# Image contrast on one core: one tile for six buffers, a first tile in two pieces, two double loads

## The chip, the cores and the metric

The kernel runs on one core of a Trainium2 chip. The metric is the device time of one execution in microseconds (us), as the median of several runs. TensorE (PE) multiplies matrices, VectorE (DVE) and ScalarE (ACT) work on rows of data, GpSimd (POOL) sets constants here, and SyncE (SP) only issues transfers. Transfers between the chip's memory and the on-chip buffers are carried by 16 DMA engines, which all issuing engines share. On-chip data lie in 128 partitions.

## The reference

The input is a batch of 16 images with 3 planes of 512 x 512 float32 values. Each of the 48 planes is pulled away from its own mean by a factor and clipped:

```python
def reference(x, factor):                      # x: (16, 3, 512, 512), factor 1.5
    mean = np.mean(x, axis=(2, 3), keepdims=True)
    return np.clip(mean + factor * (x - mean), 0, 1).astype(np.float32)
```

Every value is read once and written once: 50.33 MB in and 50.33 MB out. The mean of a plane must be known before its first value can be written.

## The kernel before

**Tiling.** The input is seen as a flat row of numbers, cut into rows of 8192 (`ROW`, 32 KB). One plane fills 32 such rows. A tile is 128 rows, one per partition, so it holds 4 whole planes and 4 MiB (4.194 MB). There are 12 tiles, numbered from 0. Six buffers of 32 KB per partition hold them (`BUFS`, pool `xpool`; a buffer is taken in `load`, line 64).

**Load** (lines 63 to 66). SP issues one transfer per tile. The first six are issued ahead of all work (lines 100 and 101); the load of tile t + 6 is issued after the work on tile t is written down (lines 104 and 105), and waits until the store of tile t has landed, since it takes its buffer.

**Compute** (lines 68 to 94). The sum of each row is shared by two engines: DVE reduces columns 0 to 4351 (line 71), ACT copies columns 4352 to 8191 into a scratch tile and accumulates their sum on the way (line 75). Two small matmuls with a block matrix that holds (1 - factor) / (512 * 512) add the 32 rows of each plane and hand the result to all of them (lines 79 and 80); the second matmul waits for the DVE sum. DVE copies this bias out (line 82). Then the tile is rewritten in place in column pieces: ACT computes relu(factor * x + bias) (line 88), DVE takes the minimum with 1 (line 89). Tile 0 has three pieces of 2048, 3072 and 3072 columns (`FIRST`), every other tile two of 5120 and 3072 (`CHUNKS`).

**Store** (lines 96 and 97). ACT issues the stores. Tile 0 is stored in three transfers: its first 2048 columns, written down after the second piece, then 3072 and 3072 columns. Every other tile is stored by one transfer after its last piece. ACT's queue is in order, so a store that waits also holds back the ACT work on the next tile.

**What sets the order.** The kernel is written in Tile, a layer that derives the waits between engines and transfers from the tiles that they touch; `manual_schedule` keeps the order in which the instructions are written down on each engine. SP's queue holds only the loads, ACT's queue the activations and the stores. Both queues of transfers run on the same 16 DMA engines. A transfer of a tile is cut by rows: one packet per row and partition, 32 KB for whole rows, 8 or 12 KB for the pieces of tile 0's stores.

Of the kernel before, what the change touches and what calls it, by code (L numbers as in the profile page):

```python
# [1 line left out]

# [4 lines left out]


P = 128  # L10
ROW = 8192
BUFS = 6
CHUNKS = (5120, 3072)
FIRST = (2048, 3072, 3072)
SUM = 4352


@with_exitstack
def kernel(
    ctx: ExitStack,  # L20
    tc: tile.TileContext,
    x: bass.AP,
    factor: float,
    out: bass.AP,
):


    nc = tc.nc
    f32 = mybir.dt.float32
    Alu = mybir.AluOpType  # L30
    Act = mybir.ActivationFunctionType

    B, C, H, W = x.shape
    n_img, n_pix = B * C, H * W
    ppi = n_pix // ROW
    per_tile = P // ppi
    n_tiles = n_img // per_tile
    assert ppi * ROW == n_pix and per_tile * n_tiles == n_img

    factor = float(factor)  # L40
    wconst = (1.0 - factor) / float(n_pix)

    x_f = x.rearrange("b c h w -> (b c h w)")
    out_f = out.rearrange("b c h w -> (b c h w)")

    def dram(ap, t, c0=0, c1=ROW):
        return bass.AP(tensor=ap.tensor, offset=t * P * ROW + c0, ap=[[ROW, P], [1, c1 - c0]])

    consts = ctx.enter_context(tc.tile_pool(name="consts", bufs=1))
    xpool = ctx.enter_context(tc.tile_pool(name="xpool", bufs=BUFS))  # L50
    jpool = ctx.enter_context(tc.tile_pool(name="jpool", bufs=1))
    rpool = ctx.enter_context(tc.tile_pool(name="rpool", bufs=2))
    bpool = ctx.enter_context(tc.tile_pool(name="bpool", bufs=2))
    psum = ctx.enter_context(tc.tile_pool(name="psum", bufs=2, space=bass.MemoryType.PSUM))

    blockw = consts.tile([P, P], f32, name="blockw")
    nc.gpsimd.memset(blockw, 0.0)  # L57
    for a in range(0, P, ppi):
        nc.gpsimd.memset(blockw[a : a + ppi, a : a + ppi], wconst)  # L59

    tiles = {}

    def load(t):
        xt = xpool.tile([P, ROW], f32, name="xt")
        nc.sync.dma_start(out=xt, in_=dram(x_f, t))  # L65
        tiles[t] = xt

    def compute(t):
        xt = tiles[t]
        sums = rpool.tile([P, 2], f32, name="sums")  # L70
        nc.vector.tensor_reduce(  # L71
            out=sums[:, 0:1], in_=xt[:, 0:SUM], axis=mybir.AxisListType.X, op=Alu.add
        )
        junk = jpool.tile([P, ROW - SUM], f32, name="junk")
        nc.scalar.activation(  # L75
            out=junk, in_=xt[:, SUM:ROW], func=Act.Copy, accum_out=sums[:, 1:2]
        )
        pbias = psum.tile([P, 1], f32, name="pbias")
        nc.tensor.matmul(pbias, blockw, sums[:, 1:2], start=True, stop=False)  # L79
        nc.tensor.matmul(pbias, blockw, sums[:, 0:1], start=False, stop=True)  # L80
        bias = bpool.tile([P, 1], f32, name="bias")
        nc.vector.tensor_copy(out=bias, in_=pbias)  # L82

        chunks, pieces = (FIRST, True) if t == 0 else (CHUNKS, False)
        c, done = 0, 0
        for n in chunks:
            part = xt[:, c : c + n]
            nc.scalar.activation(out=part, in_=part, func=Act.Relu, bias=bias, scale=factor)  # L88
            nc.vector.tensor_scalar(out=part, in0=part, scalar1=1.0, scalar2=None, op0=Alu.min)  # L89
            if pieces and c > 0:  # L90
                store(t, done, c)
                done = c
            c += n
        store(t, done, ROW)

    def store(t, c0, c1):
        nc.scalar.dma_start(out=dram(out_f, t, c0, c1), in_=tiles[t][:, c0:c1])  # L97

    with tc.manual_schedule():
        for t in range(min(BUFS, n_tiles)):  # L100
            load(t)
        for t in range(n_tiles):
            compute(t)
            if t + BUFS < n_tiles:
                load(t + BUFS)


# [1 line left out]
_INS = ['x', 'factor']  # L109
_OUTS = [((16, 3, 512, 512), 'float32')]  # L110

_NUMBERS = {'factor': 1.5}


# [26 lines left out]
```

## Time and profile before

| | |
|---|---|
| median of 6 runs | 240.02 us (239.57 to 240.24) |
| profiled execution | 239.52 us, of which the profile's span is 237.3 us |
| traffic | 100.67 MB, mean 424 GB/s over the span |
| ACT busy | 131.2 us (55%) |
| DVE busy | 111.9 us (47%) |
| PE busy | 14.0 us (6%) |
| load queue (q1) | 1728 packets, 12 transfers of 4096 KB |
| store queue (q10) | 2016 packets, 11 transfers of 4096 KB, 2 of 1536 KB, 1 of 1024 KB |

The span runs from the first to the last instruction of the profiled execution. Times inside it are counted from its start. Some 2.2 us of the execution lie around the span. Busy shares of engines are means over the whole span; a share of the DMA engines counts all 16. A transfer's issue and its landing are far apart, because transfers queue: a load lands a median of 33.9 us after its issue, a store of a whole tile 50.4 us after it. The packets include 16 small ones per transfer that report its completion, which is why 12 loads of 128 rows make 1728 packets.

### The profile page before, as it was taken

The page shows a single profiled execution, that of the slowest core. Times are in us where ns is not written, and L with a number is a line of the kernel's source. Part 1 is how long each engine was busy: PE and PEld are TensorE (multiplying, and loading weights), DVE is VectorE, ACT ScalarE, POOL GpSimd, SP SyncE. Part 2 cuts the span into 40 slices and gives each one's busy share as a digit, 9 for nine tenths or more (in the row PEclk, how much of TensorE's full clock was granted, in tenths as well). Part 3 has the DMA queues.
Part 4 walks back from the last instruction along what each step waited for, and adds up shares of the span by engine and source line. Part 5 has one row for each costly group of instructions (what it writes and reads, how often), then busy time and mean ns, then how long its engine had stood idle before and what let it go on. Part 6 is the DMA issues. An engine that isn't in the chain of part 4 may idle for free.

```text
span 237.3 us, 310 instructions
## 1 busy us (share of the span) xinstructions
PE 14.0 (6%) x48; PEld 12.0 (5%) x48; DVE 111.9 (47%) x49; ACT 131.2 (55%) x50; POOL 0.9 (0%) x9
## 2 busy tenths in 40 slices
PE   0000010100101001010010010001001001000000
PEld 0000010100101001010010010001001001000000
DVE  0072855919468293782764282562734627330000
ACT  2058678586785967769379059256536806900000
POOL 1000000000000000000000000000000000000000
DMA  7999998989999999999999999999999999999996
GB/s 265 442 442 442 420 447 379 472 387 447 453 442 425 420 392 442 442 442 442 442 442 442 436 405 409 431 442 442 442 442 436 442 442 403 425 414 442 442 442 265
DMA packets 3745, 100.67 MB, mean 424 GB/s; under 512 B 416, under 2 KB 416, under 8 KB 416
## 3 DMA queue, kind: packets, MB, share of 16 engines
q1 hardware_dynamic: 1728, 50.33, 49.6%
q10 hardware_dynamic: 2016, 50.33, 49.2%
q14 instruction: 1, 0.01, 0.0%
HBM read 50.33 MB, written 50.33 MB: 424 GB/s over the span
## 4 chain that ended last, share of the span: by engine, by line
DMA 39%; another core or an unknown queue 24%; DVE 12%; ACT 10%; issue 2%; PE 1%; SPq 0%; ACTq 0%
DMA xt<-in_x_dram 19%; DMA out_dram<-xt 19%; ACT xt L88 9%; DVE xt L89 6%; DVE sums L71 5%; ACT junk L75 1%; PE pbias L80 1%; SPq L65 0%; PE pbias L79 0%; DVE bias L82 0%; ACTq L97 0%; ACTq L88 0%; ACTq L75 0%
## 5 line engine op out<-in xcount | busy, mean ns | idle before, releaser
L88 ACT ACTIVATE xt<-xt,bias 128x3072 f32<-128x3072 f32 (+2 forms) x25 | 87.9, 3566 | 21.0 <-DVE bias L82 13.6
L89 DVE TENSOR_SCALAR xt<-xt 128x3072 f32<-128x3072 f32 (+2 forms) x25 | 54.3, 2208 | 56.1 <-ACT xt L88 56.1
L71 DVE TENSOR_REDUCE sums<-xt 128x1 f32<-128x4352 f32 x12 | 56.2, 4682 | 33.8 <-DMA xt<-in_x_dram 33.8
L75 ACT ACTIVATE junk<-xt 128x3840 f32<-128x3840 f32 x12 | 40.9, 3404 | 55.3 <-DMA xt<-in_x_dram 41.8
L79 PE MATMUL pbias<-sums,blockw 128*128 128x1 f32 x24 | 7.0, 361 | 183.7 <-ACT junk L75 183.7
L79 PEld LDWEIGHTS pbias<-sums,blockw 128*128 128x128 f32 x24 | 6.0, 310 | 184.7 <-ACT junk L75 167.9
L80 PE MATMUL pbias<-sums,blockw 128*128 128x1 f32 x24 | 7.0, 362 | 2.9 <-DVE sums L71 2.5
L80 PEld LDWEIGHTS pbias<-sums,blockw 128*128 128x128 f32 x24 | 6.0, 311 | 3.9 <-DVE sums L71 3.4
L82 DVE COPY bias<-pbias 128x1 f32<-128x1 f32 x12 | 1.9, 158 | 8.1 <-PE pbias L80 8.1
L75 ACT ACTIVATION_READ_ACCUMULATOR junk<-xt 128x1 f32 x12 | 2.3, 188 | 0.0
L75 ACT ACT_TABLE_LOAD x1 | 1.3, 1283 | 0.7 <-PEq L122 0.7
L59 POOL MEMSET blockw<- 32x32 f32 x4 | 0.5, 118 | 0.2
L57 POOL MEMSET blockw<- 128x128 f32 x1 | 0.2, 204 | 0.3 <-POOLq L122 0.3
L122 POOL MEMSET const-bfloat16-1.0<- 128x1 bf16 x1 | 0.1, 111 | 0.0
L122 POOL MEMSET const-uint8-127<- 128x1 uint8 x1 | 0.1, 111 | 0.0
L122 POOL MEMSET const-float32-1.0<- 128x1 f32 x1 | 0.1, 108 | 0.0
L122 POOL MEMSET const-float32-0.0<- 128x1 f32 x1 | 0.1, 103 | 0.2 <-issue 0.2
## 6 DMA issues: line engine op xcount, KB each, us to landing
xt<-in_x_dram SPq DMA_DIRECT2D x12, 4096.0 KB, 33.9
out_dram<-xt ACTq DMA_DIRECT2D x11, 4096.0 KB, 50.4
out_dram<-xt ACTq DMA_DIRECT2D x2, 1536.0 KB, 30.8
out_dram<-xt ACTq DMA_DIRECT2D x1, 1024.0 KB, 15.4
```

The costliest lines, as they stand in the source:

```text
L57: nc.gpsimd.memset(blockw, 0.0)
L59: nc.gpsimd.memset(blockw[a : a + ppi, a : a + ppi], wconst)
L71: nc.vector.tensor_reduce(out=sums[:, 0:1], in_=xt[:, 0:SUM], axis=mybir.AxisListType.X, op=Alu.add)
L75: nc.scalar.activation(out=junk, in_=xt[:, SUM:ROW], func=Act.Copy, accum_out=sums[:, 1:2])
L79: nc.tensor.matmul(pbias, blockw, sums[:, 1:2], start=True, stop=False)
L80: nc.tensor.matmul(pbias, blockw, sums[:, 0:1], start=False, stop=True)
L82: nc.vector.tensor_copy(out=bias, in_=pbias)
L88: nc.scalar.activation(out=part, in_=part, func=Act.Relu, bias=bias, scale=factor)
L89: nc.vector.tensor_scalar(out=part, in0=part, scalar1=1.0, scalar2=None, op0=Alu.min)
L122: nc = _bacc.Bacc("TRN2", target_bir_lowering=False, num_devices=1)
```

## The change

The six buffers become one tile `ring` of 128 x 6 x 8192 values, and tile t uses its part t modulo 6. `load` takes a range of columns and a number of tiles. Tile 0 is loaded by two transfers, columns 0 to 2047 (8 KB per row) and 2048 to 8191 (24 KB per row). Tile 1 is loaded by one transfer as before. Tiles 2 and 3 come with one transfer of 8 MiB, tiles 4 and 5 with another; tiles 6 to 11 with one each as before. Tile 0 is stored by two transfers with the same cut as its load; the first of them stands where it stood, and the second, of 24 KB per row, comes after the last piece. The arithmetic, the pieces in which it is done and all other stores are as before. There are 11 loads and 13 stores in place of 12 and 14.

```diff
-FIRST = (2048, 3072, 3072)
+SHORT = 2048
+FIRST = (SHORT, 3072, 3072)
...
-    xpool = ctx.enter_context(tc.tile_pool(name="xpool", bufs=BUFS))
+    xpool = ctx.enter_context(tc.tile_pool(name="xpool", bufs=1))
...
-    tiles = {}
-    def load(t):
-        xt = xpool.tile([P, ROW], f32, name="xt")
-        nc.sync.dma_start(out=xt, in_=dram(x_f, t))
-        tiles[t] = xt
+    ring = xpool.tile([P, BUFS, ROW], f32, name="ring")
+    def load(t, c0=0, c1=ROW, n=1):
+        b = t % BUFS
+        src = bass.AP(
+            tensor=x_f.tensor,
+            offset=t * P * ROW + c0,
+            ap=[[ROW, P], [P * ROW, n], [1, c1 - c0]],
+        )
+        nc.sync.dma_start(out=ring[:, b : b + n, c0:c1], in_=src)
     def compute(t):
-        xt = tiles[t]
+        xt = ring[:, t % BUFS, :]
...
-        chunks, pieces = (FIRST, True) if t == 0 else (CHUNKS, False)
-        c, done = 0, 0
-        for n in chunks:
+        c = 0
+        for n in FIRST if t == 0 else CHUNKS:
             part = xt[:, c : c + n]
             nc.scalar.activation(out=part, in_=part, func=Act.Relu, bias=bias, scale=factor)
             nc.vector.tensor_scalar(out=part, in0=part, scalar1=1.0, scalar2=None, op0=Alu.min)
-            if pieces and c > 0:
-                store(t, done, c)
-                done = c
+            if t == 0 and c == FIRST[0]:
+                store(t, 0, c)
             c += n
-        store(t, done, ROW)
+        store(t, FIRST[0] if t == 0 else 0, ROW)
     def store(t, c0, c1):
-        nc.scalar.dma_start(out=dram(out_f, t, c0, c1), in_=tiles[t][:, c0:c1])
+        nc.scalar.dma_start(out=dram(out_f, t, c0, c1), in_=ring[:, t % BUFS, c0:c1])
     with tc.manual_schedule():
-        for t in range(min(BUFS, n_tiles)):
-            load(t)
+        load(0, c1=SHORT)
+        load(0, c0=SHORT)
+        load(1)
+        load(2, n=2)
+        load(4, n=2)
         for t in range(n_tiles):
             compute(t)
             if t + BUFS < n_tiles:
                 load(t + BUFS)
```

## The prediction

> **What bounds the kernel now.** I read the page's rates first, because this kernel does little arithmetic for 100.67 MB of traffic.
>
> ```profile
> span 237.3 us, 310 instructions
> ...
> DMA  7999998989999999999999999999999999999996
> GB/s 265 442 442 442 420 447 379 472 387 447 453 442 425 420 392 442 442 442 442 442 442 442 436 405 409 431 442 442 442 442 436 442 442 403 425 414 442 442 442 265
> ...
> q1 hardware_dynamic: 1728, 50.33, 49.6%
> q10 hardware_dynamic: 2016, 50.33, 49.2%
> ```
>
> The reader is to see that the 16 DMA engines are busy in every slice but the first and the last: 49.6% of loads and 49.2% of stores make 98.8% of the span. ACT is at 55% and DVE at 47%. The slices scatter, since a packet is counted where it starts, so I asked for the rate in long stretches. Columns: the stretch, the busy time of PE, PEld, DVE, ACT and POOL, the clock, the DMA share, GB/s.
>
> ```profile
> 25.00:65.00 40.00, 3.52 (x12) 3.00 (x12) 25.24 (x12) 28.54 (x12) 0.00 (x0) 1.00 1.01 429
> 100.00:195.00 95.00, 5.86 (x20) 5.00 (x20) 47.77 (x21) 54.05 (x20) 0.00 (x0) 1.00 1.00 433
> ```
>
> 433 GB/s is the working rate, with one load and one store beside each other. 100.67 MB at 433 is 232.5 us. The remaining 4.8 us of the span are: about 1.4 lost in the first 2.5 us (197 GB/s there, 0.59 MB short), 1.0 at the end (the last store, issued at 210.06, lands 26.3 later at 236.3; the span ends at 237.3), 0.4 in the stretch 25 to 65 (4 GB/s times 40 us is 0.16 MB), and small pieces of a few tenths. So a change of order can win at most this little; it loses wherever both DMA queues run empty.
>
> Next, how the two queues share, by single stores' time from issue to landing (one line from each of three answers for the store's line, with the landing under it).
>
> ```profile
> L97 ACTq DMA_DIRECT2D out_dram<-xt x1: 374/374/374, 22.0 to 22.0; - x1
> DMA to landing us min/median/max: 15.4/15.4/15.4
> L97 ACTq DMA_DIRECT2D out_dram<-xt x1: 339/339/339, 25.2 to 25.2; - x1
> DMA to landing us min/median/max: 25.6/25.6/25.6
> L97 ACTq DMA_DIRECT2D out_dram<-xt x1: 338/338/338, 28.0 to 28.0; - x1
> DMA to landing us min/median/max: 36.1/36.1/36.1
> ```
>
> The three pieces of tile 0 land at 37.4, 50.8 and 64.1. So 1.573 MB (12 KB of each row) took 13.4 and 13.3 us: 117 to 118 GB/s. Store 1, with whole rows of 32 KB, was issued at 42.6 and landed 40.9 later, at 83.5: 4.194 MB in 19.4 us, 216 GB/s. Both are what alternation of one row's piece per queue gives: 433 x 12/(12+32) = 118, 433 x 32/64 = 216. I use this rule; for 8 KB it gives 87, and 1.049 MB in 12.1 us, so that store 0's first piece moved from 25.3 to 37.4.
>
> Last, the pace of a tile and what holds a store back.
>
> ```profile
> 42.50 4.68 DVE L71 TENSOR_REDUCE sums<-xt 128x1 f32<-128x4352 f32 x1
> 57.25 0.34 ACTq L97 DMA_DIRECT2D out_dram<-xt  x1
> 127.70 4.51 DVE L89 TENSOR_SCALAR xt<-xt 128x5120 f32<-128x5120 f32 x2 [4.69 <-ACT xt L88]
> 136.85 4.68 DVE L71 TENSOR_REDUCE sums<-xt 128x1 f32<-128x4352 f32 x1 [4.65 <-DMA xt<-in_x_dram]
> 136.90 0.34 ACTq L97 DMA_DIRECT2D out_dram<-xt  x1
> 210.06 0.34 ACTq L97 DMA_DIRECT2D out_dram<-xt  x1
> ```
>
> A tile takes 14.75 us from its first reduction to the issue of its store (42.50 to 57.25), less than the 19.4 in which the DMA moves one tile in and one out. The store of tile 7 was ready at 132.2 and went out at 136.9, when load 8 landed: a store can wait for a load with which it shares no data. Store 11 goes out at 210.06; store 10 lands at 226.7. The last store is thus queued 16.6 us before its turn. That reserve is what the change must not use up.
>
> **The change part by part.** Named l0 to l11 for loads and s0 to s11 for stores by tile (from 0).
>
> *First load in two pieces.* SP issues one more transfer (0.37 to 0.53 us each among the first loads, in the shadow of 4 us of data that the first megabyte brings at 433 GB/s less the start). The first reduction reads columns 0 to 4351 and the activation 4352 to 8191, so both need the second piece: tile 0 starts at 13.1 as now. Later loads queue behind; none is late by more than the issue, and SP is ahead of the DMA. Cost 0; with the cover gone, 0.5 us. I see no gain either: nobody starts on the first piece.
>
> *Store of tile 0 in two pieces, not three.* One ACT issue of 0.34 us goes. The 24 KB piece is issued at 28.0, not its first half at 25.2. At both times s0's first piece still moves (to 37.4), so nothing runs empty. Packets: 128 rows more are cut on the load side, 128 fewer on the store side: 0. Completion packets: two transfers fewer, 32 of 416 small ones: 0. What moves is the sharing: from 37.4 the store gets 433 x 24/56 = 186 GB/s and the loads 247. s0 is out at 37.4 + 3.146/0.186 = 54.3, not 64.1.
>
> *Loads l2+l3 and l4+l5 as one transfer each.* Two SP issues fewer (0.42 to 0.53 us, hidden). Tile 2 now lands with tile 3. Loads by then: 22.8 to 25.3 alone, 1.08 MB; to 37.4 at 346 GB/s, 4.19 MB; the last 3.12 of 8.39 MB at 247 take 12.6 us: l2+l3 land at 50.0. Tile 2 starts at 50.0, not 42.5: 7.5 us late. Who waits: ACT and DVE, then s2, issued at 64.8. The store queue meanwhile has s1 (issued 42.6, moving 54.3 to 73.7), so the 7.5 us cost nothing; without that cover they still cost nothing in DMA time while loads are queued. l4+l5: 1.07 MB until 54.3, 7.32 MB at 216.5: 88.1. Tile 3 is done at 79.5, tile 4 starts 8.6 us later, s4 goes out at 102.9, s5 at 117.6.
>
> *Rest, 19.4 us a tile on each queue.* l6 waits for s0 (54.3) and moves 88.1 to 107.5; l7 to l11 land at 126.9, 146.3, 165.7, 185.1, 204.5. Their slots are free long before: s1 to s5 are out at 73.7, 93.1, 112.5, 131.9 and 151.3, so SP always has a load queued. Stores: s6 170.7, s7 190.1; s8 has 3.1 MB out at 204.5 and then the whole rate: 207.0, s9 216.7, s10 226.4. Tile 11 starts at 204.5 and s11 goes out at 219.3, 7.1 us before its turn, and lands at 236.1. Now it is 236.3. The reserve falls from 16.6 to 7.1 us and the end stays.
>
> *One tile for the buffers.* No instruction changes shape. A gain or a loss could only come from added waits: see the rivals. Its nearest row is the pieces of one buffer now: s0's first piece went out at 21.96, 0.03 us after the last operation on its columns (20.70 + 1.23), while other columns of the same tile were still being written. Columns are told apart inside a tile, so I take 0.
>
> *What no row shows.* How a two-tile load fares per byte: between the 429 of the cut rows and the 433 of whole ones, so 0.4 us either way over 40 us; I take 0, since its rows stay 32 KB. (Should both rows of a partition move as one piece of 64 KB, loads would get two thirds of the rate while the pair lasts, lead the stores by more, and leave a larger reserve; the sum stays.) The start: the same issue and the same first read; between nothing and -0.5 or +0.5 us (one issue); I take 0.
>
> Sum: 0 on a span of 237.3. The profiled execution took 239.52, 2.2 around the span and 0.50 under the median; the other runs scatter from 239.57 to 240.24. I predict the median, **240.0**.
>
> *A rule against the change.* The long stretches hold 433 GB/s with rows 32 KB apart within one load. The Trainium skill, "DMA: Bandwidth & Descriptors", section "Latency and other measured facts", reports that copies whose per-partition rows lie 4 MiB apart fell to 103 GB/s. The double load steps 4 MiB, though only between a partition's two rows. At 103 GB/s its two transfers would take 163 us where 433 gives 39: an estimate from that page of up to 124 us more; no run here shows it yet.
>
> *A rule for a gain.* Through ten tile boundaries between 100 and 195 us the rate stays 433: queued transfers pay nothing for beginning. The same page, section "Anatomy of one DMA", fits a fixed 2 us to each (on another issue path). Two transfers fewer would make 4 us of gain by it, and 0 by the row, which I follow.
>
> **The rivals.**
>
> *A late last store (slower).* Transfers wait for others: s7 above, and one load waited 19.6 us for another load. With 24 transfers in place of 26 the pairs shift. If s9 had to wait for l11, ACT would stand until 204.5: tile 10 ends at 219.2, 2.5 us after s9 is out, and s11 goes out at 233.9, lands 9.7 us later at 243.6: +7.3, about 247.3. It decides once tile 10 starts after 226.4 - 29.5 = 196.9. Against it: s6 and s7 each wait for the very next load now, which ACT needs anyway. Chance 0.10.
>
> *The buffers are no longer told apart (slower).* Were every touch of the one tile ordered, a tile would cost load 9.7 + 14.75 + store 9.7 = 34 us; twelve make 410. The row of s0 speaks against it. 0.03.
>
> *The double loads run slow (slower).* Until 88.1 the two move beside the stores. If all traffic from 22.8 on then ran at 379 GB/s, the lowest slice in the middle, its 28.3 MB would take 74.6 us for 65.3: +9.3, 249.3. The decisive point is a loss of 0.48 us, 0.7% of that stretch. Against it: the low slices stand beside slices of 447 and 472, so they are the scatter of the count. 0.04.
>
> *A real gain.* Without the 0.4 us of the stretch 25 to 65 and an issue's 0.5 at the start: 239.1. For it: that stretch is where the cut rows are. Against: they stay cut. 0.09.
>
> **How the numbers follow.** No change has 0.74, in its own range 239.4 to 240.7 (0.4 us of rate, and the scatter of the runs). 0.2% is 0.48 us, about what a measurement here tells from no change; of the 0.74 I give 0.04 to faster and 0.05 to slower. Faster: 0.09 + 0.04 = 0.13. Slower: 0.10 + 0.03 + 0.04 + 0.05 = 0.22. Same: 0.65. The range 239.1 to 241.1 leaves out nearly all of the three slower rivals (0.17) and a little of the gain.
>
> **What would show it.** After: 433 GB/s from 65 to 195; first reduction at 13.1; the 24 KB store landing near 54; tile 2 starting near 50 and tile 4 near 88; the last load landing near 204 and s11 issued near 219, still before s10 lands. The prediction is wrong if a slice in the middle drops for more than one packet's scatter, if s11 is issued after s10 has landed, or if the first packets come sooner.

## The result

The changed kernel takes 239.27 us (median of 32 runs, 239.0 to 239.92), the kernel before 239.70 (median of 67 runs in the same comparison, 239.52 to 240.73). The ratio is 0.9982, with a 95% interval of 0.9977 to 0.9988: 0.43 us less between the medians. That is inside the 0.2% that the forecast called no change, at 240.0 us in a range of 239.1 to 241.1, yet it is resolved from zero, so there is a small gain to explain.

The profile of the changed kernel, first the page's rates and queues:

```profile
span 238.0 us, 307 instructions
...
DMA  7999999999999999999999999999999999999994
GB/s 308 396 441 441 418 441 410 405 441 441 441 441 435 441 435 441 413 418 413 441 441 441 435 441 441 441 431 435 424 413 413 441 441 441 441 441 435 441 435 193
...
q1 hardware_dynamic: 1840, 50.33, 49.5%
q10 hardware_dynamic: 1872, 50.33, 49.0%
```

The DMA engines are again busy from the second slice to the last but one. The packets have moved as counted: 112 more on the load queue (128 more rows, one transfer fewer), 144 fewer on the store queue (128 rows and one transfer). The profiled execution took 239.90 us, which is one of the longest of its 32, so its span must not be set against the 237.3 of before.

In the two long stretches (columns as before: busy times, clock, DMA share, GB/s):

```profile
25.00:65.00 40.00, 2.35 (x8) 2.01 (x8) 21.27 (x10) 22.94 (x10) 0.00 (x0) 1.00 1.02 432
100.00:195.00 95.00, 7.03 (x24) 6.01 (x24) 53.04 (x24) 62.93 (x24) 0.00 (x0) 1.00 1.00 432
```

The rate is 432 GB/s in both, where it was 429 and 433. The double loads, which move from 22.4 to 86.2 us and so fill the whole first stretch, go as fast as single ones.

The new order, in the timeline of the changed kernel: the first reductions of tiles 0, 2, 4 and 11, and the last store's issue.

```profile
12.78 4.69 DVE L78 TENSOR_REDUCE sums<-ring 128x1 f32<-128x4352 f32 x1 [12.78 <-DMA ring<-in_x_dram]
...
49.38 4.68 DVE L78 TENSOR_REDUCE sums<-ring 128x1 f32<-128x4352 f32 x1 [7.12 <-DMA ring<-in_x_dram]
...
86.22 4.69 DVE L78 TENSOR_REDUCE sums<-ring 128x1 f32<-128x4352 f32 x1 [7.49 <-DMA ring<-in_x_dram]
...
203.37 4.68 DVE L78 TENSOR_REDUCE sums<-ring 128x1 f32<-128x4352 f32 x1 [4.65 <-DMA ring<-in_x_dram]
...
218.10 0.34 ACTq L101 DMA_DIRECT2D out_dram<-ring  x1
```

DVE stands still for 7 us ahead of tiles 2 and 4, waiting for the second tile of a pair that it doesn't need yet, and the last store goes out 8 us later than before. None of this is in the time. Store landings, from single answers for the store's line:

```profile
L101 ACTq DMA_DIRECT2D out_dram<-ring x1: 337/337/337, 27.7 to 27.7; - x1
DMA to landing us min/median/max: 28.0/28.0/28.0
L101 ACTq DMA_DIRECT2D out_dram<-ring x1: 338/338/338, 198.7 to 198.7; - x1
DMA to landing us min/median/max: 28.8/28.8/28.8
L101 ACTq DMA_DIRECT2D out_dram<-ring x1: 338/338/338, 218.1 to 218.1; - x1
DMA to landing us min/median/max: 19.1/19.1/19.1
```

The 24 KB store of tile 0 lands at 55.7, store 10 at 227.5, store 11 at 237.2. Store 11 is queued 9.4 us before its turn.

### The profile page after: what moved, and what is told of

The parts are those of the page before. It is cut to its first block, busy times and chain, and to the rows that moved or that the text cites. A ratio compares the mean times of both kernels' runs of the same rounds, so it can differ in the third digit from the quotient of the medians.

```text
span 238.0 us, 307 instructions
## 1 busy us (share of the span) xinstructions
PE 14.1 (6%) x48; PEld 12.0 (5%) x48; DVE 112.0 (47%) x49; ACT 131.2 (55%) x50; POOL 0.9 (0%) x9
## 4 chain that ended last, share of the span: by engine, by line
DMA 57%; DVE 19%; ACT 10%; another core or an unknown queue 3%; issue 1%; PE 1%; SPq 1%; ACTq 0%
DMA ring<-in_x_dram 40%; DMA out_dram<-ring 16%; ACT ring L93 10%; DVE ring L94 9%; DVE sums L78 9%; PE pbias L87 1%; SPq L73 1%; DVE bias L89 0%; ACTq L93 0%
## 5 line engine op out<-in xcount | busy, mean ns | idle before, releaser
L93 ACT ACTIVATE ring<-ring,bias 128x3072 f32<-128x3072 f32 (+2 forms) x25 | 87.9, 3566 | 22.1 <-DVE bias L89 13.1
L94 DVE TENSOR_SCALAR ring<-ring 128x3072 f32<-128x3072 f32 (+2 forms) x25 | 54.3, 2208 | 56.1 <-ACT ring L93 56.1
L78 DVE TENSOR_REDUCE sums<-ring 128x1 f32<-128x4352 f32 x12 | 56.2, 4683 | 41.8 <-DMA ring<-in_x_dram 41.8
L82 ACT ACTIVATE junk<-ring 128x3840 f32<-128x3840 f32 x12 | 40.9, 3405 | 62.3 <-DMA ring<-in_x_dram 49.0
L82 ACT ACTIVATION_READ_ACCUMULATOR junk<-ring 128x1 f32 x12 | 2.3, 188 | 0.0
## 6 DMA issues: line engine op xcount, KB each, us to landing
out_dram<-ring ACTq DMA_DIRECT2D x1, 1024.0 KB, 16.6
```

The costliest lines, as they stand in the source:

```text
L78: nc.vector.tensor_reduce(out=sums[:, 0:1], in_=xt[:, 0:SUM], axis=mybir.AxisListType.X, op=Alu.add)
L82: nc.scalar.activation(out=junk, in_=xt[:, SUM:ROW], func=Act.Copy, accum_out=sums[:, 1:2])
```

## The experiments

Two questions: what makes the 0.43 us, and is it really the reserve of the last store that decides? For the first, START says that short first rows let data flow earlier (the first reduction stands at 12.78 us, 0.33 earlier). MERGE says that fewer transfers are cheaper. STORE says that tile 0's store in larger pieces is. Ratios are to the kernel before, with 95% intervals. The ratios are given as recorded; they are not the quotients of the medians to the last digit.

### The parts one at a time

*First load cut* (`split_load`, on the kernel before):

```diff
-        nc.sync.dma_start(out=xt, in_=dram(x_f, t))
+        cut = (0, 2048, ROW) if t == 0 else (0, ROW)
+        for c0, c1 in zip(cut, cut[1:]):
+            nc.sync.dma_start(out=xt[:, c0:c1], in_=dram(x_f, t, c0, c1))
```

> The kernel before with one edit: tile 0 is loaded in two pieces of 8 and 24 KB per row. Theory START (the gain is that the first rows are short, so that data flow earlier): the first reduction starts near 12.75 us in place of 13.1, and the time falls by about 0.35 to 0.45 us against the kernel before, ratio 0.998 to 0.9987. Theory MERGE (the gain comes from fewer transfers) and theory STORE (from tile 0's 24 KB store): the time stays, ratio 1.000.

Measured: 239.59 us, 0.9990 (0.9980 to 1.0001); first reduction at 12.97.

*First load whole* (`whole_load`, on the changed kernel):

```diff
-        load(0, c1=SHORT)
-        load(0, c0=SHORT)
+        load(0)
```

> The changed kernel with tile 0 loaded whole again; everything else of the change stays. START: the gain is gone, ratio to the kernel before 1.000 (within 0.0007), first reduction at 13.1 us. MERGE or STORE: the gain stays, 0.998.

Measured: 239.64 us, 0.9999 (0.9990 to 1.0008); first reduction at 12.95, not at 13.1.

*Store of tile 0 in two pieces* (`two_stores`, on the kernel before):

```diff
-            if pieces and c > 0:
+            if pieces and done == 0 and c > 0:
```

> The kernel before with one edit: tile 0 is stored in two pieces of 8 and 24 KB per row, not in three. START and MERGE: ratio 1.000, the last store is issued some microseconds later than 210.06 because stores get a larger share after 37 us. STORE: 0.998.

Measured: 239.68 us, 0.9998 (0.9989 to 1.0007); last store issued at 219.85.

*One tile and double loads alone* (`double_only`, on the kernel before, with the changed kernel's `ring` and `load`, and the three stores of tile 0 kept):

```diff
-        for t in range(min(BUFS, n_tiles)):
-            load(t)
+        load(0)
+        load(1)
+        load(2, n=2)
+        load(4, n=2)
```

> The kernel before with one tile for the buffers and the double loads of tiles 2-3 and 4-5; tile 0 loaded whole and stored in three pieces. START and STORE: ratio 1.000. MERGE: 0.998. If the double step of 4 MiB cost rate, above 1.002.

Measured: 239.62 us, 0.9999 (0.9990 to 1.0008); last store issued at 207.79.

What follows: taking away the cut of the first load takes away the gain, and neither MERGE nor STORE makes one alone. The reserve, too, has an owner. The last store's issue in `two_stores` and in `double_only`:

```profile
219.85 0.34 ACTq L97 DMA_DIRECT2D out_dram<-xt  x1
207.79 0.34 ACTq L102 DMA_DIRECT2D out_dram<-ring  x1
```

In the kernel before it stood at 210.06, 16.6 us before store 10 landed. With the 24 KB store alone store 10 lands at 227.3 and 7.5 us are left; with the double loads alone it lands at 226.8 and 19.0 us are left. It is the larger row of the store, which by the sharing rule takes a larger share of the engines early on, that eats the reserve; the double loads even add to it.

### Pairs, a repeat, and a thinner first piece

`split_two` is `split_load` with the edit of `two_stores`. `split_double` is `double_only` with the first load in two pieces. `after_again` is the changed kernel. `thin_first` is the changed kernel with this edit:

```diff
-        load(0, c1=SHORT)
-        load(0, c0=SHORT)
+        load(0, c1=512)
+        load(0, c0=512)
```

> The changed kernel once more, beside the pairs. The single parts gave 0.9990 (first load in two pieces), 0.9998 (store in two pieces), 0.9999 (double loads) and 0.9999 (both without the first load's cut); their product is 0.9987. If the parts only ADD, this comes out at 0.9985 to 0.999. If the 0.9982 of before holds, two parts work together (PAIR).

> The kernel before with the first load and tile 0's store both in two pieces of 8 and 24 KB per row; six buffers, single loads. ADD: 0.9985 to 0.9992. PAIR with the store: 0.998 to 0.9984. No gain from the start at all: 1.000.

> The kernel before with one tile for the buffers, the first load in two pieces and the double loads; tile 0 stored in three pieces. ADD: 0.9985 to 0.9992. PAIR with the double loads: 0.998 to 0.9984. No gain from the start at all: 1.000.

> The changed kernel, with a first load piece of 2 KB per row instead of 8 (the second is 30 KB); the stores stay. START (short first rows let data flow earlier): as good as the changed kernel or up to 0.15 us better, first reduction at 12.6 to 12.8 us. If the start plays no part: equal to the kernel with tile 0 loaded whole, 0.9999 against the kernel before.

| kernel | first load cut | median us | ratio (interval) | median span of its runs, us | profiled run less its span, us |
|---|---|---|---|---|---|
| before | no | 239.70 | 1 | 237.5 | 2.19 |
| two_stores | no | 239.68 | 0.9998 (0.9989 to 1.0007) | 237.5 | 2.22 |
| double_only | no | 239.62 | 0.9999 (0.9990 to 1.0008) | 237.4 | 2.21 |
| whole_load | no | 239.64 | 0.9999 (0.9990 to 1.0008) | 237.4 | 2.19 |
| split_load | yes | 239.59 | 0.9990 (0.9980 to 1.0001) | 237.8 | 1.89 |
| split_two | yes | 239.43 | 0.9988 (0.9977 to 0.9999) | 237.6 | 1.82 |
| split_double | yes | 239.43 | 0.9988 (0.9979 to 0.9997) | 237.6 | 1.86 |
| thin_first | yes | 239.54 | 0.9993 (0.9985 to 1.0002) | 237.7 | 1.83 |
| after_again | yes | 239.33 | 0.9993 (0.9984 to 1.0001) | 237.5 | 1.85 |
| after | yes | 239.27 | 0.9982 (0.9977 to 0.9988) | 237.4 | 1.86 |

The kernel before has 239.70 in the result's comparison and 239.66 and 239.65 in the two of the other rows; its span here is the median in each of those two, and all spans of that column are recorded to 0.1 us. Every kernel of this table with the cut lies at 0.9982 to 0.9993, every one without at 0.9998 or above. Three of the six intervals still touch 1, and the same program gave 0.9982 and 0.9993, so the size is known only to about 0.1 to 0.4 us. No pair shows more than the cut alone (0.9988 twice), so none is needed, though the intervals do not exclude PAIR by themselves. START falls. The first reductions with the cut stand between 12.78 and 13.00, and `whole_load`, without the cut and without the gain, has 12.95. The first packets start at 1.74 to 1.76 us in every kernel of the table. The thinner piece brings nothing more.

The last column says where to look instead. It is the part of an execution that lies outside the profile's span, before its first instruction or after its last. It is 2.19 to 2.22 us without the cut and 1.82 to 1.89 with it, in the profiled run of every kernel of this case (in all 32 runs of the changed kernel, 1.78 to 1.90). Take it off the medians, and the spans that remain are 237.51 for the kernel before, 237.41 for the changed one and 237.48 for its repeat: the work itself did not become shorter by anything that these runs resolve. In `split_load` and `thin_first` it even became longer: their spans have a mean of 237.78 and 237.70 us, against 237.54 and 237.52 in the runs of the kernel before beside them. What the cut takes off outside the span is there in part given back inside; why, these runs do not show. In the trace, a last 8 KB fetch on the instruction queue begins 1.67 to 1.70 us after the span without the cut and 1.18 to 1.22 after it with the cut, which points to the part behind the last instruction. The fetch moves by some 0.5 us and the time by 0.3 to 0.4, so it is a sign and not the whole account.

Besides the load's own issue and packets, the cut changes one instruction. The first reduction needs both pieces, and its second wait becomes an instruction of its own on DVE's sequencer. The reduction's line in the changed kernel, by line (operations with their count, durations in ns, first and last start):

```profile
L78 DVE TENSOR_REDUCE sums<-ring x12: 4677/4685/4687, 12.8 to 203.4; 128x1 f32<-128x4352 f32 x12
L78 DVEq EVENT_SEMAPHORE  x1: 21/21/21, 12.7 to 12.7; - x1
```

and in `whole_load`, where the second line is missing:

```profile
L78 DVE TENSOR_REDUCE sums<-ring x12: 4677/4683/4687, 12.9 to 202.6; 128x1 f32<-128x4352 f32 x12
its engine sat idle before it (us, times) until:
```

DVE has 62 recorded instructions in every kernel with the cut and 61 in every one without, while the counts of ACT and SP differ within both groups. That the extra instruction moves the end of the program, by where its code falls, fits this, but was not tried, and it is not told apart from the extra load. One dummy wait on DVE in the kernel before would tell.

### How much lateness the end allows

The summing activation of the last tile alone was repeated two or four times, with results that nobody uses, in the changed kernel and in the kernel before (`late_after_2`, `late_after_4`, `late_before_4`):

```diff
+        for _ in range(4 if t == n_tiles - 1 else 0):
+            nc.scalar.activation(out=junk, in_=xt[:, SUM:ROW], func=Act.Copy)
         pbias = psum.tile([P, 1], f32, name="pbias")
```

> The changed kernel with two more passes of the summing activation on the last tile alone, whose results nobody uses: 2 x 3.4 us on ACT before tile 11 is rewritten, so its store goes out near 218.1 + 6.8 = 224.9 us, still before store 10 lands (227.6). RESERVE (an engine's delay costs nothing until the last store is issued after the one before it has landed): time as the changed kernel, 239.3 to 239.7. If compute counted, +6.8: 246.

> The same with four passes: 13.6 us, the last store goes out near 231.7, 4.1 us after store 10 has landed. RESERVE: +4.1 us, and up to 2 us more for the start of a transfer on an empty queue: 243.5 to 245.7. If compute counted in full, +13.6: 253. If it counted nothing, 239.5.

> The kernel before with the same four passes on the last tile: its last store goes out near 210.1 + 13.6 = 223.7, before store 10 lands (226.7). RESERVE: no change, 239.6 to 240.0. If the reserve is not what matters, as late as in the changed kernel: 243.5 to 245.7.

Measured: `late_after_2` 239.33 us, 0.9985 (0.9976 to 0.9995), as the changed kernel. `late_after_4` 243.05 us, 1.0136 (1.0121 to 1.0150). `late_before_4` 239.89 us, 1.0005 (0.9995 to 1.0016). The same 13.7 us of extra ACT work cost 3.7 us in the changed kernel (243.05 against 239.33 in `late_after_2`) and nothing that is resolved in the kernel before. The last store's issue in `late_before_4`:

```profile
221.84 0.34 ACTq L99 DMA_DIRECT2D out_dram<-xt  x1
```

That is still 5.6 us before store 10 lands (227.4). In `late_after_2` it is issued at 222.50, 4.6 us before store 10 lands (227.1). In the timeline and the landings of `late_after_4`:

```profile
206.24 13.71 ACT L86 ACTIVATE junk<-ring 128x3840 f32<-128x3840 f32 x4
...
229.11 0.34 ACTq L103 DMA_DIRECT2D out_dram<-ring  x1
```

```profile
L103 ACTq DMA_DIRECT2D out_dram<-ring x1: 338/338/338, 198.0 to 198.0; - x1
DMA to landing us min/median/max: 28.7/28.7/28.7
L103 ACTq DMA_DIRECT2D out_dram<-ring x1: 338/338/338, 229.1 to 229.1; - x1
DMA to landing us min/median/max: 11.1/11.1/11.1
```

Store 10 lands at 226.7, and store 11 is issued 2.4 us after that. It then takes 11.1 us, where a queued whole tile takes 9.7 (227.5 to 237.2 in the changed kernel): 1.4 us for starting on an idle queue. 2.4 + 1.4 = 3.8, measured 3.7. The issue came 2.6 us earlier than expected: for 2.0 us the extra passes run while ACT would have waited for the bias, and 0.7 us is that tile 11 started at 202.66 here and at 203.37 in the profile of the changed kernel. RESERVE holds in these three kernels: lateness is free up to the landing of the store before, and paid in full from there.

### A version meant to be better

`split_one_store` is `split_load` with tile 0's store in one transfer:

```diff
-        chunks, pieces = (FIRST, True) if t == 0 else (CHUNKS, False)
+        chunks, pieces = (FIRST, False) if t == 0 else (CHUNKS, False)
```

> The kernel before with the first load in two pieces and tile 0's store whole (one transfer, issued near 28 us). No store row is cut. START alone: 0.9988 to 0.9993 like the other kernels with a cut first load. If the small losses of rate between 25 and 65 us come from the cut store rows, they go as well, up to 0.45 us more: 0.997 to 0.9985. If an early store matters to the end: above 1.000.

Measured: 240.08 us, 1.0013 (1.0004 to 1.0022), so it is slower than the kernel before, although its time outside the span is the short one (1.83): the spans of its runs have a median of 238.25 us, against 237.5 in the kernel before and 237.8 in `split_load`. No improvement came; of the three cases, the one above 1.000 did. The reserve is not the reason, since the last store goes out at 223.71, 3.7 us before store 10 lands (227.4). The rate in two stretches of `split_one_store`:

```profile
28.00:36.00 8.00, 1.17 (x4) 1.00 (x4) 4.60 (x2) 6.12 (x3) 0.00 (x0) 1.00 0.97 356
24.00:46.00 22.00, 1.17 (x4) 1.00 (x4) 15.65 (x7) 15.91 (x6) 0.00 (x0) 1.00 1.01 414
```

and in the same two of `split_load`:

```profile
28.00:36.00 8.00, 1.17 (x4) 1.00 (x4) 4.57 (x2) 6.15 (x3) 0.00 (x0) 1.00 1.01 426
24.00:46.00 22.00, 1.17 (x4) 1.00 (x4) 15.65 (x7) 15.91 (x6) 0.00 (x0) 1.00 1.01 425
```

Here the first store is issued at 27.9 us, and its first packets start at 32.5, whole rows beside loads of whole rows; the rate is 356 GB/s over 8 us, where `split_load` has 426. Part of that is the scatter of packets counted where they start; over 24 to 46 us, 11 GB/s less make 0.24 MB, or 0.56 us at 433, against 0.49 us between the two kernels' medians. That count still scatters: `double_only` has 417 in the same stretch and loses no time, and over 24 to 66 us the two kernels have 423 and 424. With the bytes of each packet spread over its recorded duration, `split_one_store` is 0.8 us of data at 433 GB/s behind `split_load` at 36 us and 0.5 us behind at 66 and at 195 us. The two profiled spans differ by only 0.14 us in the end (237.95 and 237.81), so that the dip makes the half microsecond of the medians fits, but is not shown. The kernel before has 426 from 28 to 36 us too, the changed one and `double_only` 410, all with a first store of 8 KB rows. Whether the size of the first store's rows or the moment at which it comes makes the dip wasn't separated.

## Why the prediction was right, and where it was not

**The bound.** "433 GB/s is the working rate" held (432 after), and with both queues filled to the end the change of order had little to win inside the span. The prediction's account of the 4.8 us beyond the pure transfer time is short: its three items make 2.8 us, and the other 2.0 are not "a few tenths". The same view of the kernel before has 275 GB/s from 2.5 to 5 us, a loss of 0.9 us, and 422 from 195 to 236, a loss of 1.0. The first megabyte at 433 GB/s is 2.4 us of data, not 4, which still covers an issue of 0.5. Neither slip enters the sum.

**The replay.** Its times, worked out from 433 GB/s shared by the size of the rows, against the profile:

| step | predicted us | measured us |
|---|---|---|
| tile 0 starts | 13.1 | 12.78 |
| tile 0 stored | 54.3 | 55.7 |
| tile 2 starts | 50.0 | 49.38 |
| tile 4 starts | 88.1 | 86.22 |
| load 11 landed | 204.5 | 203.37 |
| store 11 issued | 219.3 | 218.10 |
| store 10 landed | 226.4 | 227.5 |
| reserve | 7.1 | 9.4 |
| store 11 landed | 236.1 | 237.2 |

The sharing rule thus carries 200 us with an error of 2 us; the reserve, a difference of two of its times, came out 2.3 us larger. The last landing is 1.1 us late in an execution that was long for this kernel.

**The pieces at zero.** Fewer transfers: 0, measured 0.9999 (`double_only`). The store in two pieces: 0, measured 0.9998 (`two_stores`), and its effect on the reserve was put in the right place. The one tile with its added waits: 0, contained in `double_only`.

**The rule on rows 4 MiB apart.** By the prediction's estimate from the Trainium skill, "DMA: Bandwidth & Descriptors", section "Latency and other measured facts", up to 124 us more were possible. The double loads ran at 432 GB/s. Here a partition's own two rows are 4 MiB apart and neighbouring partitions stay 32 KB apart, so what the page describes was not met. The fixed 2 us per transfer that the same page, section "Anatomy of one DMA", fits for transfers issued by GpSimd do not show here while transfers are queued, as the row had said. On an idle queue `late_after_4` paid 1.4.

**The rivals.** A late last store: the mechanism is real, and `late_after_4` gave its price (the lateness plus 1.4 us, where the prediction left out the 1.4), but the waits between transfers did not pair that badly here. Buffers not told apart and slow double loads: excluded by 432 GB/s and `double_only`. A real gain: it came, 0.1 to 0.4 us, and not from the rate or the issue, which were the reasons given for it. That the measured 239.27 lies close to that rival's 239.1 is luck.

**What was off.** The forecast lay 0.73 us above the measured median. 0.3 of that was there before the change: 240.02, on which it stands, is the median of six runs, and 67 runs give 239.70. The other 0.43 is the change, and the term behind it is "The profiled execution took 239.52, 2.2 around the span", taken over unchanged into the sum. That term measured 1.86 us after the change. The prediction also said of the first load's cut that it would cost 0, "I see no gain either: nobody starts on the first piece": right for the data (the first reduction came 0.33 us earlier in one profile, and no span shows it), but with the cut came a wait more on DVE and less time outside the span. Whether the one causes the other stays open.

## What to carry to other kernels

Where the DMA engines are busy from end to end, work out first when the last store is issued against the landing of the store before it; while that difference is positive a late last tile costs nothing, and beyond it the shortfall and the start of an idle queue are paid (here 2.4 and 1.4 us). It does not vouch for the rate earlier on: `split_one_store` kept a reserve of 3.7 us and was slower. When a change of some tenths of a microsecond is to be explained, take the profile's span off the execution's time in every kernel first: here all of the gain that is resolved lay outside the span, and a plausible story about early data inside it was wrong. Then group kernels by the part that they have, since single intervals of 0.1% were too wide to tell one from the next.

## What the runs showed of the hardware that was not expected

The two queues shared the 16 engines as if by turns of one row each, so that their rates stood as the row sizes do: with store rows of 8, 12, 24 and 32 KB against loads of 32 KB the landings came within 2 us of this rule. An execution's time outside the profile's span is not a constant of the chip: 2.19 to 2.22 us or 1.82 to 1.89 in the profiled runs, by kernel. A first store of whole rows beside a running stream of whole-row loads went with 356 GB/s over 8 us, in place of 410 to 426, in a kernel whose span was 0.45 us longer than that of `split_load`; that the one makes the other is not shown.
